# Streaming x through one core: main tiles of 128 positions of 4 batches in one loop over five groups, and a jump to a new instruction block at the start of the VectorE and ACT programs

## The chip, the cores and the metric

The kernel runs on one core of one Trainium2 chip. The metric is the time of one execution in device microseconds (us). The kernel before takes 630.12 us (median of 3 runs, 630.04 to 630.36). The profile is one execution recorded by the hardware profiler. Its span, from the first to the last instruction of the program, is about 2 us shorter than the time of the same run.

Names in the profile: DVE is VectorE, ACT is ScalarE, POOL is GpSimd, PE is TensorE (PEld its weight loads), SP is the engine that issues the DMAs of x; SPq and ACTq are DMA issues by SP and ACT. A packet is one contiguous piece that a DMA engine moves. The packet records do not name the engine, so a figure "for each DMA engine" is the total over 16.

## The reference

```python
def setup_inputs():
    B, S, D = 8, 2048, 4096
    return {"x": np.random.randn(B, S, D).astype(np.float32),
            "w": np.random.randn(D, 1).astype(np.float32)}

def reference(x, w):
    proj = (x @ w).squeeze(-1)                    # (8, 2048)
    cm = np.maximum.accumulate(proj, axis=1)      # running maximum along a row
    is_record = (proj >= cm).astype(np.float32)
    return np.cumsum(is_record, axis=1).astype(np.float32)
```

x is 268.4 MB and is read once. The output is 64 KB. Each element of x is used in one multiplication and one addition.

## The kernel before

Every position needs a dot product of 4096 elements. VectorE takes columns 0 to 2815 of a row in one instruction; POOL multiplies the other 1280 columns by w and ACT adds them up. A main tile is 8 MB: 128 partitions, each with four rows (64 KB) that follow each other in memory. There are three such buffers. The last 128 positions come as small pieces at the end, the tail pieces. SP issues a tile's DMA when VectorE and ACT have both finished the tile that was in its buffer before.

```python
    RS = (4, 4, 4, 3)            # rows of a partition in each of four groups
    R = RS[0]
    NS = 3                       # main buffers
    NG = len(RS); NL = NG - 1
    N = R * P                    # 512 positions in a group
    STARTS = [sum(RS[:g]) * P for g in range(NG)]
    S0 = sum(RS) * P             # the last 128 positions come as small pieces
    ...
        for g in range(NG):
            r = RS[g]
            for t in range(B):                       # one tile per batch
                i = SY.dma_start(
                    out=at(g, t)[:, : r * D],
                    in_=x[B - 1 - t, STARTS[g] : STARTS[g] + r * P, :].rearrange(
                        "(p r) d -> p (r d)", r=r
                    ),
                ).then_inc(xs[t], 16)
                u, n = user_before(g, t)
                if n:
                    i._wait_ge(*(free(u, n)))        # the buffer is free
                if g == t == 0:
                    A.dma_start(out=w_row, in_=...).then_inc(ws, 16)
    ... (small pieces of the last 128 positions, constants, broadcast of w by TensorE)

        def group_dots(r, g=0):                      # VectorE
            for t in range(B):
                b, xb = B - 1 - t, at(g, t)
                for j in range(r):
                    i = dot(xb[:, j * D : j * D + VC], w_v[:, :VC],
                            sum_v[:, j * B + b : j * B + b + 1])
                    if j == 0:
                        i._wait_ge(xs[t], 16)
                i.then_inc(fr[t], 1)

        with V.Fori(0, NL):
            group_scans(); V.sem_inc(psr, -3); group_dots(R)
        group_scans(); V.sem_inc(psr, -3); group_dots(RS[-1], NL)

        def group_products(r, g=0):                  # POOL, one instruction a row
            for t in range(B):
                for j in range(r):
                    xl = at(g, t)[:, j * D + VC : (j + 1) * D]
                    i = G.tensor_mul(out=xl, in0=xl, in1=w_sb).then_inc(pl, 1)
                    ...
        def group_sums(r, g=0):                      # ACT, each row waits for its product
            for t in range(B):
                for j in range(r):
                    i = add_up(at(g, t)[:, j * D + VC : (j + 1) * D], ...)._wait_ge(pl, j + 1)
                i.then_inc(fr[t], 1)
                A.sem_inc(pl, -r)
            ...
        def group_rows(r):                           # TensorE: sums to rows of the batches
            ...
            for j in range(r):
                for k, l in enumerate((sum_p, sum_v)):
                    i = T.matmul(out=ps[:B, j : r * P : r], lhsT=l[:, j * B : (j + 1) * B],
                                 rhs=identity, start=k == 0, stop=k == 1)
```

## Time and profile before

| | read from | value |
|---|---|---|
| time | timed runs | 630.12 us |
| span | page | 629.3 us |
| DMA queue 1, share of 16 engines' span | queue table | 98.9% |
| VectorE, POOL, ACT busy | page, part 1 | 65%, 59%, 29% |
| one 64 KB packet, median | packet records of the trace | 2.418 us |
| first x packet starts, last one ends | packet records | 1.98 us, 623.75 us |
| from the last x packet to the span's end | difference | 5.5 us |
| issue to landing of an 8 MB tile, median | DMA table | 45.0 us |

A tile is 128 packets of 64 KB on 16 DMA engines, so eight packets in a row on each: 8 x 2.418 = 19.34 us. The whole of x at the median packet times is 619.85 us for each engine. The stream as it ran is 621.8 us.

The lines below are from the page of the kernel before: busy time and share of the span of each engine; the DMA row of the 40 slices (9 is 90% busy or more); the queue table; the chain that ended last; three groups of instructions (busy us and mean ns of one, then idle us before them and what ended it); and the DMA issues (count, us from issue to landing).

```profile
span 629.3 us, 1140 instructions
...
PE 29.1 (5%) x96; PEld 13.5 (2%) x96; DVE 407.3 (65%) x294; ACT 181.2 (29%) x274; POOL 370.7 (59%) x149
...
DMA  9999999999999999999999999999999999999996
...
q1 hardware_dynamic: 6544, 268.50, 98.9%
...
DMA 16%; POOL 3%; DVE 2%; issue 1%; PE 1%; ACT 0%; SPq 0%
...
L124 DVE CUSTOM_DVE_ANT_0 xall<-xall,w_v 128x2816 f32<-128x2816 f32 (+1 forms) x129 | 385.5, 3041 | 181.8 <-DMA xall<-in_x_dram 181.8
L276 POOL TENSOR_TENSOR xall<-xall,w_sb 128x1280 f32<-128x1280 f32 x120 | 345.0, 2909 | 246.7 <-DMA xall<-in_x_dram 243.3
L130 ACT ACTIVATE xall<-xall 128x1280 f32<-128x1280 f32 (+2 forms) x130 | 162.9, 1253 | 428.6 <-POOL xall L276 408.3
...
xall<-in_x_dram SPq DMA_DIRECT2D x24, 45.0
```

The DMA row and the queue table say what bounds this kernel: the 16 engines are busy nearly all the time. The row alone would not show a short stop: e9 below stops for 1.6 us and has the same row. The packet records settle it, with 621.6 us busy of 621.8. The groups say that VectorE and POOL spend most of their idle time waiting for exactly these DMAs. The chain gives DMA only 16%, because it starts at 484 us and follows buffers through the engines that release them; it does not tell how full the queue is. The last line tells that: a tile lands 45.0 us after its issue and needs 19.3 us itself, so it was queued about 25.7 us ahead of its turn. I call this the lead: issue to landing, less 19.34 us.

The next lines are from the timeline of the kernel before, at the start (start us, us, engine, line, operation, count, idle time before and what ended it), and from one tile in the middle of the first group.

```profile
0.91 0.60 ACTq L178 DMA_DIRECT2D w<-in_w_dram  x1
...
0.97 1.34 SPq L168 DMA_DIRECT2D xall<-in_x_dram  x3
...
2.62 2.07 PE L224 MATMUL ps<-w,identity 8*128 8x512 f32 x2 [2.62 <-DMA w<-in_w_dram]
...
22.80 3.09 DVE L124 CUSTOM_DVE_ANT_0 xall<-xall,w_v 128x2816 f32<-128x2816 f32 x1 [0.67 <-DMA xall<-in_x_dram]
22.85 8.63 POOL L276 TENSOR_TENSOR xall<-xall,w_sb 128x1280 f32<-128x1280 f32 x3 [20.85 <-DMA xall<-in_x_dram]
```

```profile
81.65 3.09 DVE L124 CUSTOM_DVE_ANT_0 xall<-xall,w_v 128x2816 f32<-128x2816 f32 x1 [7.52 <-DMA xall<-in_x_dram]
81.69 11.49 POOL L276 TENSOR_TENSOR xall<-xall,w_sb 128x1280 f32<-128x1280 f32 x4 [8.13 <-DMA xall<-in_x_dram]
84.63 1.27 ACT L130 ACTIVATE xall<-xall 128x1280 f32<-128x1280 f32 x1 [9.67 <-POOL xall L276]
...
93.22 1.27 ACT L130 ACTIVATE xall<-xall 128x1280 f32<-128x1280 f32 x1 [1.50 <-POOL xall L276]
...
94.61 0.33 SPq L168 DMA_DIRECT2D xall<-in_x_dram  x1
```

w is there at 2.62 us, ahead of x. The first dot starts when the first tile has landed. In the middle of the run a tile starts its dots at 81.65, and SP issues the next DMA for that buffer at 94.61: 13 us from landing to reuse.

### The profile page before, as it was taken

How to read it: one execution, taken by the hardware profiler on the slowest of the kernel's cores; microseconds unless marked ns; L12 is line 12 of the kernel's file. 1: busy time of each engine (PE TensorE's matmuls, PEld its weight loads, DVE VectorE, ACT ScalarE, POOL GpSimd, SP SyncE). 2: the span in 40 equal slices, each digit the busy share in tenths (PEclk: the TensorE clock that was granted, in tenths of full speed). 3: DMA queues.
4: the chain of work that ended last, by engine and by line, in shares of the span. 5: the costliest groups of instructions: out<-in, count | busy, mean ns of one | idle time of the engine just before them, and what ended most of it. 6: DMA issues, size and time to landing. Idle time of an engine off the chain costs nothing. (4 is left out here: it accounts for less than half of the span.)

```text
span 629.3 us, 1140 instructions
## 1 busy us (share of the span) xinstructions
PE 29.1 (5%) x96; PEld 13.5 (2%) x96; DVE 407.3 (65%) x294; ACT 181.2 (29%) x274; POOL 370.7 (59%) x149
## 2 busy tenths in 40 slices
PE   8000000000020000000001000000002000000100
PEld 3000000000010000000000000000001000000000
DVE  0755775556766567755578655676556976655897
ACT  1222332223322233222233222332223232232254
POOL 0554675456765557745577555676557666555775
PEclk9999999999999999999996555555555555555565
DMA  9999999999999999999999999999999999999996
GB/s 401 400 467 400 446 421 425 442 437 429 442 425 450 417 450 417 459 408 458 408 458 408 458 408 458 408 459 408 462 418 438 416 447 441 413 447 444 404 425 248
DMA packets 6563, 268.54 MB, mean 427 GB/s; under 512 B 760, under 2 KB 1016, under 8 KB 1568
## 3 DMA queue, kind: packets, MB, share of 16 engines
q1 hardware_dynamic: 6544, 268.50, 98.9%
q10 hardware_dynamic: 16, 0.02, 0.0%
q14 instruction: 3, 0.02, 0.0%
HBM read 268.45 MB, written 0.07 MB: 427 GB/s over the span
## 5 line engine op out<-in xcount | busy, mean ns | idle before, releaser
L124 DVE CUSTOM_DVE_ANT_0 xall<-xall,w_v 128x2816 f32<-128x2816 f32 (+1 forms) x129 | 385.5, 3041 | 181.8 <-DMA xall<-in_x_dram 181.8
L276 POOL TENSOR_TENSOR xall<-xall,w_sb 128x1280 f32<-128x1280 f32 x120 | 345.0, 2909 | 246.7 <-DMA xall<-in_x_dram 243.3
L130 ACT ACTIVATE xall<-xall 128x1280 f32<-128x1280 f32 (+2 forms) x130 | 162.9, 1253 | 428.6 <-POOL xall L276 408.3
L312 PE MATMUL ps<-identity,small 128*8 128x128 f32 x60 | 13.0, 406 | 568.6 <-PEq L309 568.6
L130 ACT ACTIVATION_READ_ACCUMULATOR xall<-xall 128x1 f32 x130 | 24.2, 186 | 0.0
L336 POOL TENSOR_TENSOR xall<-xall,w_sb 128x1280 f32<-128x1280 f32 (+2 forms) x8 | 21.1, 2632 | 3.1 <-DMA xall<-in_x_dram 3.0
L312 PEld LDWEIGHTS ps<-identity,small 128*8 128x8 f32 x60 | 7.3, 125 | 575.4 <-issue 571.3
L140 DVE TENSOR_TENSOR_SCAN cm<-ps,cm,small 8x512 f32<-8x512 f32 (+3 forms) x8 | 7.0, 869 | 18.8 <-PE ps L312 18.4
L224 PE MATMUL w_v<-w,identity 8*128 8x512 f32 x14 | 12.1, 1056 | 0.0
L124 DVE DVE_READ_ACCUMULATOR2_ANT small<- 128x1 f32 x133 | 10.8, 81 | 0.0
L246 DVE MEMSET ps<- 8x512 f32 x1 | 0.5, 485 | 15.7 <-ACT w L235 15.7
L146 DVE TENSOR_TENSOR_SCAN cnt<-ps,cnt,small 8x512 f32<-8x512 f32 (+3 forms) x8 | 7.0, 870 | 0.3
L224 PEld LDWEIGHTS w_v<-w,identity 8*128 8x128 f32 x14 | 4.6, 332 | 7.3 <-issue 7.3
L143 DVE TENSOR_TENSOR ps<-ps,cm 8x512 f32<-8x512 f32 (+3 forms) x8 | 3.9, 487 | 0.3
L232 ACT COPY w_sb<-w_v 128x768 f32<-128x768 f32 x1 | 0.8, 799 | 11.4 <-PE w_v L224 11.4
L347 POOL TENSOR_TENSOR masked<-fold,small 128x4 f32<-128x4 f32 x8 | 1.6, 201 | 3.2 <-DVE small L124 3.2
L124 DVE CUSTOM_DVE_ANT_0 xall<-xall,w_v,small 128x480 f32<-128x480 f32 (+2 forms) x4 | 3.1, 810 | 0.2 <-DVE small L124 0.2
L357 PE MATMUL ps<-fold,masked 128*8 128x32 f32 x20 | 2.0, 235 | 25.3 <-ACT masked L352 17.7
L352 ACT ACTIVATE masked<-fold,small 128x4 f32<-128x4 f32 x10 | 3.0, 298 | 0.3
L336 POOL TENSOR_TENSOR xall<-xall,w 128x640 f32<-128x640 f32 (+1 forms) x2 | 2.3, 1137 | 0.1
L224 PE MATMUL ps<-w,identity 8*128 8x512 f32 x2 | 2.1, 1135 | 2.6 <-DMA w<-in_w_dram 2.6
L231 ACT ACT_TABLE_LOAD x1 | 1.3, 1283 | 2.7 <-DVE fold L242 2.7
(18 smaller groups left out, 5.3 us busy)
## 6 DMA issues: line engine op xcount, KB each, us to landing
xall<-in_x_dram SPq DMA_DIRECT2D x8, 6144.0 KB, 33.5
xall<-in_x_dram SPq DMA_DIRECT2D x6, 2048.0 KB, 42.4
xall<-in_x_dram SPq DMA_DIRECT2D x1, 1264.0 KB, 36.6
xall<-in_x_dram SPq DMA_DIRECT2D x1, 816.0 KB, 39.3
xall<-in_x_dram SPq DMA_DIRECT2D x1, 784.0 KB, 37.9
xall<-in_x_dram SPq DMA_DIRECT2D x2, 240.0 KB, 26.6
xall<-in_x_dram SPq DMA_DIRECT2D x1, 416.0 KB, 39.4
xall<-in_x_dram SPq DMA_DIRECT2D x24, 45.0
```

The source lines that it names most:

```text
L124: return V.tensor_tensor_reduce(out=xsl, in0=xsl, in1=wsl, scale=1.0, scalar=seed, op0=ALU.mult, op1=ALU.add, accum_out=dst,)
L130: return A.activation(out=xsl, in_=xsl, func=ACTF.Copy, accum_out=dst)
L140: V.tensor_tensor_scan(out=cm_, data0=src, data1=low, initial=cm0, op0=ALU.max, op1=ALU.max,)._wait_ge(psr, base).then_inc(psr, 1)
L143: V.tensor_tensor(out=src, in0=src, in1=cm_, op=ALU.is_ge)._wait_ge(psr, base + 1).then_inc(psr, 1)
L146: V.tensor_tensor_scan(out=cnt_, data0=src, data1=low, initial=cnt0, op0=ALU.add, op1=ALU.max,)._wait_ge(psr, base + 2).then_inc(cs, 1)
L224: i = T.matmul(out=dst, lhsT=identity[:NW, k : k + 1].to_broadcast([NW, P]), rhs=w_row, start=True, stop=True,).then_inc(bw, 1)
L276: i = G.tensor_mul(out=xl, in0=xl, in1=w_sb).then_inc(pl, 1)
L312: i = T.matmul(out=ps[:B, j : r * P : r], lhsT=l[:, j * B : (j + 1) * B], rhs=identity, start=k == 0, stop=k == 1,)
L336: G.tensor_mul(out=xl, in0=xl, in1=w_pool(*p))._wait_ge(xq[i], 16).then_inc(pl, 1)
L347: return eng.tensor_tensor(out=e, in0=by_b, in1=acc.to_broadcast([P, H]), op=ALU.mult)
L352: return A.activation(out=e, in_=by_b, func=ACTF.Copy, scale=acc)._wait_ge(pa, na).then_inc(ms, 1)
L357: return T.matmul(out=ps[:B, k * Q : (k + 1) * Q], lhsT=masked[:, n * B : (n + 1) * B], rhs=by_i, start=start, stop=stop,)
```

## The change

The intent: fewer and larger instructions on POOL, one loop for all main tiles instead of a loop and an unrolled rest, and instruction loops that begin at a block boundary. A main tile now holds 128 positions of four batches: partition 4q + b has rows 4q to 4q + 3 of batch b, still 64 KB of consecutive memory. A group is 384 positions of all eight batches (six tiles), and there are five groups. POOL multiplies a tile's four rows in one instruction (two and two in the last tile of a group); ACT starts after it. At a group's end POOL adds the two partial sums and spreads them with a mask, and TensorE makes rows of them with twelve small matmuls. The last main tile comes in two halves. VectorE and ACT jump to an address aligned to 128 instruction slots before anything else.

```diff
-    RS = (4, 4, 4, 3)
-    R = RS[0]
+    R = 4
     NS = 3
-    NG = len(RS)
+    H = 4
+    NC = 3
+    NT = NC * B // H
+    N = NC * P
+    NG = 5
+    STARTS = [g * N for g in range(NG)]
+    S0 = NG * N
...
+    for eng in (V, A):
+        eng.addr_align(128, 0, max_nops=0)
...
         for g in range(NG):
-            r = RS[g]
-            for t in range(B):
-                i = SY.dma_start(
-                    out=at(g, t)[:, : r * D],
-                    in_=x[B - 1 - t, STARTS[g] : STARTS[g] + r * P, :].rearrange(
-                        "(p r) d -> p (r d)", r=r
-                    ),
-                ).then_inc(xs[t], 16)
+            for t in range(NT):
+                b0, s0 = t % 2 * H, STARTS[g] + t // 2 * P
+                src = x[b0 : b0 + H, s0 : s0 + P, :].rearrange(
+                    "b (q r) d -> q b (r d)", r=R
+                )
...            (last tile of the last group: two halves, semaphores xs[t] and xh)
+                    i = SY.dma_start(out=at(t), in_=src).then_inc(xs[t], 16)
...
-                for j in range(r):
-                    xl = at(g, t)[:, j * D + VC : (j + 1) * D]
-                    i = G.tensor_mul(out=xl, in0=xl, in1=w_sb).then_inc(pl, 1)
+                rows = at(t).rearrange("p (r d) -> p r d", r=R)
+                n = R // 2 if t == NT - 1 else R
+                for j in range(0, R, n):
+                    xl = rows[:, j : j + n, VC:]
+                    i = G.tensor_mul(
+                        out=xl, in0=xl, in1=w_one.to_broadcast([P, n, PC])
+                    ).then_inc(pl, 1)
+                    landed(i, t, j)
+            G.tensor_tensor(out=sum_t, in0=sum_v, in1=sum_p, op=ALU.add)...
+            G.tensor_tensor(out=gmask..., in0=sum_t..., in1=by_b..., op=ALU.mult)...
...
-                for k, l in enumerate((sum_p, sum_v)):
+                for c in range(NC):
+                    k = j * NC + c
                     i = T.matmul(
-                        out=ps[:B, j : r * P : r], lhsT=l[:, j * B : (j + 1) * B],
-                        rhs=identity, start=k == 0, stop=k == 1,
+                        out=ps[:B, c * P + j : (c + 1) * P : R],
+                        lhsT=gmask[:, k * B : (k + 1) * B],
+                        rhs=by_i, start=True, stop=True,
                     )
```

More of the change, by code (lines that the diff above doesn't have):

```diff
@@ L41 @@
     NW = D // WC
-    RS = (4, 4, 4, 3)
-    R = RS[0]
+    R = 4
     NS = 3
-    NG = len(RS)
-    NL = NG - 1
-    N = R * P
-    STARTS = [sum(RS[:g]) * P for g in range(NG)]
-    S0 = sum(RS) * P
-    assert S0 + P == S
+    H = 4
+    Q = P // H
+    NC = 3
[4 more added lines that the diff above has]
+    S0 = NG * N
+    assert S0 + P == S and NT % NS == 0
     VC = 2816
@@ L53 @@
     CV = 3584
-    H = 4
-    Q = P // H
     LAST = [
@@ L87 @@
     w_sb = sb([P, PC], "w_sb")
-    cm = sb([B, N], "cm")
-    cnt = sb([B, N], "cnt")
+    cm = sb([B, N + P], "cm")
+    cnt = sb([B, N + P], "cnt")
+    gmask = sb([P, R * NC * B], "gmask")
     masked = sb([P, 10 * B], "masked")
@@ L102, in cut @@
         return small[:, off[0] - n : off[0]]
-    sum_v, sum_p = cut(R * B), cut(R * B)
+    sum_v, sum_p, sum_t = (cut(R * NT) for _ in range(3))
     acc_v, acc_p = cut(B - 2), cut(B - 2)
@@ L112, in sem @@
         return tc.alloc_semaphore(f"{name}_{next(ns)}")
-    xs = [sem("xs") for _ in range(B)]
-    fr = [sem("fr") for _ in range(B)]
+    xs = [sem("xs") for _ in range(NT)]
+    fr = [sem("fr") for _ in range(NT)]
     xq = [sem("xq") for _ in TILES]
-    ws, bw, wc, cs, od, oe, psr, pd, pl, go, sd, pa, con, fo, ms, p7, mg, pg, ml = (
-        sem(n) for n in "ws bw wc cs od oe psr pd pl go sd pa con fo ms p7 mg pg ml".split()
+    ws, bw, wc, cs, od, oe, psr, pd, pl, xh, sd, pa, con, fo, ms, p7, mg, pg, ml, mk = (
+        sem(n) for n in "ws bw wc cs od oe psr pd pl xh sd pa con fo ms p7 mg pg ml mk".split()
     )
@@ L148, in scans, with at, col_of @@
         )._wait_ge(psr, base + 2).then_inc(cs, 1)
-    def at(g, t):
-        return xbuf[(t if g < NL else t + NS - 1) % NS]
+    def at(t):
+        return xbuf[t % NS]
     def user_before(g, t):
-        if t >= NS:
-            return t - NS, g + 1
-        if g == NL:
-            return B - NS + t, g
-        return max(u for u in range(B) if u % NS == t), g
-    def free(u, n):
-        return (p7, n) if u == B - 1 else (fr[u], 2 * n)
+        return (t - NS, g + 1) if t >= NS else (t + NT - NS, g)
+    def free(u, n):
+        return (p7, n) if u == NT - 1 else (fr[u], 2 * n)
+    def col_of(t, j):
+        return (j * NC + t // 2) * 2 + t % 2
+    for eng in (V, A):
+        eng.addr_align(128, 0, max_nops=0)
     with tc.tile_critical(no_gpsimd_drain=True):
         for g in range(NG):
-            r = RS[g]
-            for t in range(B):
-                i = SY.dma_start(
-                    out=at(g, t)[:, : r * D],
-                    in_=x[B - 1 - t, STARTS[g] : STARTS[g] + r * P, :].rearrange(
-                        "(p r) d -> p (r d)", r=r
-                    ),
-                ).then_inc(xs[t], 16)
-                u, n = user_before(g, t)
+            for t in range(NT):
[3 more added lines that the diff above has]
+                )
+                half = R // 2 * D
+                last = t == NT - 1
+                u, n = user_before(g, t)
+                if last and g == NG - 1:
+                    i = SY.dma_start(
+                        out=at(t)[:, :half], in_=src[:, :, :half]
+                    ).then_inc(xs[t], 16)
+                    SY.dma_start(
+                        out=at(t)[:, half:], in_=src[:, :, half:]
+                    ).then_inc(xh, 16)
+                else:
+                    i = SY.dma_start(out=at(t), in_=src).then_inc(xs[t], 16)
+                    if last:
+                        SY.sem_inc(xh, 16)
                 if n:
-                    i._wait_ge(*(free(u, n)))
+                    i._wait_ge(*free(u, n))
                 if g == t == 0:
@@ L182 @@
                     SY.dma_start(
-                        out=out[:, STARTS[g - 1] : STARTS[g]], in_=cnt
+                        out=out[:, STARTS[g - 1] : STARTS[g]], in_=cnt[:, :N]
                     )._wait_ge(cs, g + 1).then_inc(od, 16)
         def slot(m):
-            if m < NS:
-                return None, xbuf[m][:, RS[-1] * D :]
-            u = B - NS if m < 2 * NS else B - NS + 1
-            return u, at(NL, u)[:, (m % NS) * D : (m % NS + 1) * D]
-        freed = {None}
+            u = NT - NS + m // 4
+            return u, at(u)[:, m % 4 * D : (m % 4 + 1) * D]
+        freed = set()
         for i, (m, c0, c1, _, _) in enumerate(TILES):
@@ L215 @@
         G.memset(masked, 0.0).then_inc(con, 1)
-        G.memset(cm[:, N - 1 :], NEG).then_inc(con, 1)
-        G.memset(cnt[:, N - 1 :], 0.0).then_inc(con, 1)
+        G.memset(cm[:, N - 1 : N], NEG).then_inc(con, 1)
+        G.memset(cnt[:, N - 1 : N], 0.0).then_inc(con, 1)
         T.wait_ge(con, 2)
@@ L246 @@
         V.memset(ps[:B, :N], LOW)._wait_ge(wc, 3).then_inc(psr, 1)
-        def group_scans(r=R):
-            n = r * P
-            scans(cm[:, :n], cnt[:, :n], ps[:B, :n], cm[:, N - 1 :], cnt[:, N - 1 :])
-        def group_dots(r, g=0):
-            for t in range(B):
-                b, xb = B - 1 - t, at(g, t)
-                for j in range(r):
-                    i = dot(
-                        xb[:, j * D : j * D + VC], w_v[:, :VC],
-                        sum_v[:, j * B + b : j * B + b + 1],
-                    )
-                    if j == 0:
-                        i._wait_ge(xs[t], 16)
-                i.then_inc(fr[t], 1)
@@ L264, with group_scans, landed @@
-        with V.Fori(0, NL):
+        def group_scans():
+            scans(
+                cm[:, :N], cnt[:, :N], ps[:B, :N], cm[:, N - 1 : N], cnt[:, N - 1 : N]
+            )
+        def landed(i, t, j):
+            if j == 0:
+                i._wait_ge(xs[t], 16)
+            elif t == NT - 1 and j == R // 2:
+                i._wait_ge(xh, 16)
+        with V.Fori(0, NG):
             group_scans()
             V.sem_inc(psr, -3)
-            group_dots(R)
-        group_scans()
-        V.sem_inc(psr, -3)
@@ L270 @@
-        group_dots(RS[-1], NL)
-        def group_products(r, g=0):
-            for t in range(B):
-                for j in range(r):
-                    xl = at(g, t)[:, j * D + VC : (j + 1) * D]
-                    i = G.tensor_mul(out=xl, in0=xl, in1=w_sb).then_inc(pl, 1)
-                    if j == 0:
-                        i._wait_ge(xs[t], 16)
-        G.wait_ge(wc, 3)
-        with G.Fori(0, NL):
-            group_products(R)
-            G.wait_ge(pg, 1).then_inc(pg, -1)
-        group_products(RS[-1], NL)
@@ L286, in group_sums @@
-        def group_sums(r, g=0):
-            for t in range(B):
-                b = B - 1 - t
-                for j in range(r):
-                    i = add_up(
-                        at(g, t)[:, j * D + VC : (j + 1) * D],
-                        sum_p[:, j * B + b : j * B + b + 1],
-                    )._wait_ge(pl, j + 1)
+            for t in range(NT):
+                xb = at(t)
+                for j in range(R):
+                    c = col_of(t, j)
+                    i = dot(
+                        xb[:, j * D : j * D + VC], w_v[:, :VC], sum_v[:, c : c + 1]
+                    )
+                    landed(i, t, j)
+                i.then_inc(fr[t], 1)
@@ new lines @@
+        G.wait_ge(wc, 3)
+        w_one = w_sb.rearrange("p (o c) -> p o c", o=1)
+        with G.Fori(0, NG):
+            for t in range(NT):
+                rows = at(t).rearrange("p (r d) -> p r d", r=R)
[5 more added lines that the diff above has]
+                    ).then_inc(pl, 1)
+                    landed(i, t, j)
+            G.tensor_tensor(
+                out=sum_t, in0=sum_v, in1=sum_p, op=ALU.add
+            )._wait_ge(fr[NT - 1], 2).then_inc(mk, 1)
+            G.tensor_tensor(
+                out=gmask.rearrange("p (k b) -> p k b", b=H),
+                in0=sum_t.rearrange("p (k o) -> p k o", o=1).to_broadcast(
+                    [P, R * NT, H]
+                ),
+                in1=by_b.rearrange("p (o b) -> p o b", o=1).to_broadcast(
+                    [P, R * NT, H]
+                ),
+                op=ALU.mult,
+            )._wait_ge(mk, 1).then_inc(mk, 1)
+            G.wait_ge(pg, 1).then_inc(pg, -1)
@@ L294, in group_sums @@
+        with A.Fori(0, NG):
+            for t in range(NT):
+                for j in range(R):
+                    c = col_of(t, j)
+                    i = add_up(
+                        at(t)[:, j * D + VC : (j + 1) * D], sum_p[:, c : c + 1]
+                    )
+                    if j == 0 or t == NT - 1 and j == R // 2:
+                        i._wait_ge(pl, 1)
+                    if j == R - 1 or t == NT - 1 and j == R // 2 - 1:
+                        A.sem_inc(pl, -1)
                 i.then_inc(fr[t], 1)
-                A.sem_inc(pl, -r)
@@ L296, in group_sums @@
             A.wait_ge(pd, 1).then_inc(pd, -1)
-        with A.Fori(0, NL):
-            group_sums(R)
-        group_sums(RS[-1], NL)
-        def group_rows(r):
-            T.wait_ge(fr[B - 1], 2).then_inc(p7, 1)
-            T.sem_inc(fr[B - 1], -2)
-            if r == R:
-                for s in xs:
-                    T.sem_inc(s, -16)
-                T.sem_inc(pg, 1)
+        with T.Fori(0, NG):
+            T.wait_ge(mk, 2).then_inc(p7, 1)
+            T.sem_inc(mk, -2)
+            T.sem_inc(fr[NT - 1], -2)
+            for s in (*xs, xh):
+                T.sem_inc(s, -16)
+            T.sem_inc(pg, 1)
@@ L309, in group_rows @@
             T.wait_ge(od, 16).then_inc(od, -16)
-            for j in range(r):
-                for k, l in enumerate((sum_p, sum_v)):
+            for j in range(R):
+                for c in range(NC):
+                    k = j * NC + c
                     i = T.matmul(
-                        out=ps[:B, j : r * P : r], lhsT=l[:, j * B : (j + 1) * B],
-                        rhs=identity, start=k == 0, stop=k == 1,
-                    )
-                    if j == r - 1:
-                        i.then_inc((pd, psr)[k], 1)
@@ L319 @@
-        with T.Fori(0, NL):
-            group_rows(R)
-        group_rows(RS[-1])
+                        out=ps[:B, c * P + j : (c + 1) * P : R],
+                        lhsT=gmask[:, k * B : (k + 1) * B],
+                        rhs=by_i, start=True, stop=True,
+                    )
+                    if k == 0:
+                        i.then_inc(pd, 1)
+            i.then_inc(psr, 1)
         nv = npool = na = 0
@@ L376 @@
             if m == 2:
-                group_scans(RS[-1])
+                group_scans()
             if m == 4:
```

## The prediction

> **What bounds the kernel now.** The DMA stream of x. The queue table gives queue 1 98.9% of the span; the slice row shows the DMA engines at 90% or more in 39 of 40 slices. In the packet records a 64 KB packet takes 2.418 us, so 16 engines move 433.7 GB/s; the Trainium skill, "DMA: Bandwidth & Descriptors", section "Where 436 GB/s comes from", puts the ceiling at 435.2, and the trace agrees. First x packet 1.98 us after the span's start, last one ended at 623.76: 621.8 us of stream, 621.6 busy. At median packet times it would take 619.9; the rest is slow packets, 0.6 us in the first ones, 1.1 us between 30 and 118 us. After the last packet 5.5 us remain: last dots, turn matmul, scans, output DMA, exit barrier. VectorE (65%), POOL (59%) and ACT (29%) are not limits.
>
> The DMA table shows 45.0 us from issue to landing of an 8 MB tile whose transfer takes 8 x 2.418 = 19.3 us: each DMA is queued 25 us before its turn.
>
> **What the change does.**
> - Same bytes. 30 tiles of 8 MB instead of 24 of 8 MB and 8 of 6 MB: 1024 packets of 48 KB (1.815 us) become 768 of 64 KB, 0.1 us less per engine. One tile is halved (32 KB packets): +0.05 us. A partition's row stays 64 KB contiguous.
> - POOL multiplies four rows in one instruction, about 4 x 2.91 = 11.6 us; ACT (1.46 us a row) starts only after it: release 17.4 us after landing instead of 13.1. Issue to landing falls from 45 to about 40.5 us, twice the 19.3 needed. No stall.
> - Group end: POOL adds and masks (under 1 us), TensorE does 12 small matmuls instead of 16 wider ones (3.2 us before), scans take about 2.6 us instead of 3.2. All inside the slack.
> - The last main tile in halves brings VectorE to the tail pieces about 3 us earlier, but the timeline shows VectorE and POOL waiting for DMA there already. No gain; the last pieces and their 5.5 us stay.
> - The jump costs VectorE and ACT a branch, possibly an instruction fetch. If ACT's small load of w slips behind the first x packets, the first dots start after 22.8 us, but need to start only by about 40. No effect.
> - SP issues three-dimensional tail pieces in 0.6 us, main tiles in 0.4: first packet up to 0.2 us later.
>
> **Prediction.** What is removed is off the critical path. Sum: -0.1, +0.05, +0.2; slow packets may change by -1.5 to +1. I expect 629.9 us, 8 in 10 between 628.7 and 631.1; faster by over 2% 0.01, within 2% 0.97, slower by over 2% 0.02.
>
> **Signs.** Right: 64 KB packets at 2.42 us, first packet at 2.0 to 2.3, stream near 621.5, 5.5 us behind it, issue to landing near 40, fewer POOL instructions. Wrong: packets over 2.45 us throughout, gaps in the slice row, VectorE idle beside tiles that have landed.
>
> **What would make it wrong.** Four batches lie 32 MB apart. The same page, section "Latency and other measured facts", reports much lower rates for row pitches of large powers of two between HBM tensors. The tail pieces already read this way at 0.611 us per 16 KB (429 GB/s), so I give it little weight. Or instruction fetches behind full queues could stall an engine near the end: some us at most.

## More of the kernel before

Most runs agree within 0.5 us.

## The result, and the profile after

The changed kernel takes 630.33 us (median of 4 runs, 630.22 to 630.45) against 630.24 us of the kernel before in the same rounds. The ratio is 1.0001, with a 95% interval of 0.9984 to 1.0018. Ratios are the mean time of one kernel's runs over that of the other's of the same rounds, so they are not quite the ratio of the medians quoted. They come out when the first run of each kernel is left out; for e6, whose runs scatter, that makes 1.0394 instead of 1.0378 with all runs.

The profiled run of before was one of its slower ones: it took 631.05 us and its span is 629.3 us, while the spans of its timed runs in the later rounds are 628.1 to 628.9. So the 1.0 us between the two profiled spans is not a gain. Nor does the granted TensorE clock matter here: it was 0.773 in this profile and 1.000 in the one after, but TensorE is busy for 5% of the span, and runs of the kernel before at 0.64 to 0.89 all took 629.9 to 630.7 us.

The lines below are from the page of the changed kernel, in the order of those of before.

```profile
span 628.3 us, 1242 instructions
...
PE 23.2 (4%) x156; PEld 12.7 (2%) x156; DVE 406.9 (65%) x297; ACT 171.7 (27%) x274; POOL 360.7 (57%) x74
...
DMA  9999999999999999999999999999999999999996
...
q1 hardware_dynamic: 6416, 268.50, 98.9%
...
DMA 71%; POOL 18%; ACT 7%; issue 2%; DVE 1%; SPq 0%; PE 0%
...
L125 DVE CUSTOM_DVE_ANT_0 xall<-xall,w_v 128x2816 f32<-128x2816 f32 (+1 forms) x129 | 385.5, 3041 | 167.7 <-DMA xall<-in_x_dram 167.7
L291 POOL TENSOR_TENSOR xall<-xall,w_sb 128x5120 f32<-128x5120 f32 (+1 forms) x35 | 332.2, 9498 | 242.1 <-DMA xall<-in_x_dram 216.8
L131 ACT ACTIVATE xall<-xall 128x1280 f32<-128x1280 f32 (+2 forms) x130 | 161.3, 1241 | 428.3 <-POOL xall L291 411.3
...
xall<-in_x_dram SPq DMA_DIRECT2D x29, 41.7
```

The DMA row and the queue share are as before. POOL has 74 instructions instead of 149; a product of four rows takes 11.05 us in the timeline, against 4 x 2.909 = 11.64 (the mean of 9498 ns mixes these with the products of two rows). The chain now gives DMA 71%, POOL 18% and ACT 7%. It reads like another kernel, but nothing of it became a limit: it follows each buffer through POOL and ACT for the whole run. Issue to landing is 41.7 us, a lead of 22.4 us instead of 25.7.

The timeline of the changed kernel, at the start and at a tile in the middle:

```profile
0.96 42.99 SPq L185 DMA_DIRECT2D xall<-in_x_dram  x4
...
1.34 2.30 ACTq L191 DMA_DIRECT2D w<-in_w_dram  x1
...
11.45 2.07 PE L235 MATMUL ps<-w,identity 8*128 8x512 f32 x2 [11.45 <-DMA w<-in_w_dram]
...
27.21 11.03 POOL L291 TENSOR_TENSOR xall<-xall,w_sb 128x5120 f32<-128x5120 f32 x1 [25.21 <-ACT w L246]
...
30.09 3.05 DVE L125 CUSTOM_DVE_ANT_0 xall<-xall,w_v 128x2816 f32<-128x2816 f32 x1
```

```profile
81.62 3.09 DVE L125 CUSTOM_DVE_ANT_0 xall<-xall,w_v 128x2816 f32<-128x2816 f32 x1 [7.25 <-DMA xall<-in_x_dram]
81.67 11.05 POOL L291 TENSOR_TENSOR xall<-xall,w_sb 128x5120 f32<-128x5120 f32 x1 [8.33 <-DMA xall<-in_x_dram]
...
92.75 1.27 ACT L131 ACTIVATE xall<-xall 128x1280 f32<-128x1280 f32 x1 [14.26 <-POOL xall L291]
...
96.52 1.25 ACT L131 ACTIVATE xall<-xall 128x1280 f32<-128x1280 f32 x1
...
97.89 0.53 SPq L185 DMA_DIRECT2D xall<-in_x_dram  x1
```

The load of w is issued at 1.34 us instead of 0.91, so after SP's first DMA of x (0.96) and no longer before it, and the issue takes 2.30 us instead of 0.60. Packets of x now go first: the packets of w move only at 8.0 us, after two packets of x, and the small packets that end the load come at 10.5 to 10.9 us, after a third. TensorE waits for them until 11.45, and the first dot starts at 30.09 us although the first tile has landed at 23.6. In the middle, the tile that starts at 81.62 is free at 97.89, after 16.3 us instead of 13.

The packet records give the sum for both kernels and for the experiments that follow (us). "Lost" is the time of the x packets above the median for their size, for each DMA engine.

| run | first x packet | lost in the first 16 packets | lost later | last x packet ends | after it | w moves at | first dot |
|---|---|---|---|---|---|---|---|
| before | 1.98 | 0.64 | 1.13 | 623.75 | 5.50 | 1.9 | 22.80 |
| after | 2.39 | 0.95 | 0.31 | 622.91 | 5.41 | 8.0 | 30.09 |
| e1, no jump | 2.37 | 0.88 | 0.22 | 623.40 | 5.49 | 1.9 | 23.80 |
| e2, jump only | 1.99 | 0.63 | 0.21 | 623.09 | 5.50 | 7.4 | 30.29 |
| e3, row products | 2.38 | 0.88 | 0.06 | 623.15 | 5.51 | 7.8 | 30.16 |
| e4, one batch a tile | 1.98 | 0.68 | 0.34 | 622.41 | 5.48 | 7.4 | 29.53 |
| e5, after again | 2.36 | 0.93 | 0.16 | 622.74 | 5.45 | 8.0 | 30.05 |

Every run is the same sum: about 2 us of start, 620 us of packets at their median, 0.8 to 1.8 us lost, 5.5 us of end. The first three add up to the end of the last packet within 0.6 us, so smaller differences than that should not be read from the table. The 6.1 us by which w is late are in none of these terms.

### The profile page after: what moved, and what is told of

It reads as the page before. It is cut to its first block, busy times and chain, and to the rows that moved or that the text cites. A ratio compares the mean times of both kernels' runs of the same rounds, so it can differ in the third digit from the quotient of the medians.

```text
span 628.3 us, 1242 instructions
## 1 busy us (share of the span) xinstructions
PE 23.2 (4%) x156; PEld 12.7 (2%) x156; DVE 406.9 (65%) x297; ACT 171.7 (27%) x274; POOL 360.7 (57%) x74
## 4 chain that ended last, share of the span: by engine, by line
DMA 71%; POOL 18%; ACT 7%; issue 2%; DVE 1%; SPq 0%; PE 0%
DMA xall<-in_x_dram 71%; POOL xall L291 18%; ACT xall L131 7%; POOL xall L357 1%; DVE xall L125 0%; SPq L185 0%; PE ps L378 0%; ACT masked L373 0%; SPq L207 0%; POOL masked L368 0%; DVE cm L141 0%; DVE cnt L147 0%; DVE ps L144 0%; SPq L463 0%; DVE small L125 0%
## 5 line engine op out<-in xcount | busy, mean ns | idle before, releaser
L291 POOL TENSOR_TENSOR xall<-xall,w_sb 128x5120 f32<-128x5120 f32 (+1 forms) x35 | 332.2, 9498 | 242.1 <-DMA xall<-in_x_dram 216.8
L335 PE MATMUL ps<-fold,gmask 128*8 128x32 f32 x120 | 7.2, 240 | 563.7 <-PEq L331 563.7
L141 DVE TENSOR_TENSOR_SCAN cm<-ps,cm,small 8x384 f32<-8x384 f32 (+2 forms) x9 | 6.9, 765 | 23.6 <-PE ps L335 23.2
L335 PEld LDWEIGHTS ps<-fold,gmask 128*8 128x8 f32 x120 | 6.5, 114 | 565.9 <-issue 565.9
L147 DVE TENSOR_TENSOR_SCAN cnt<-ps,cnt,small 8x384 f32<-8x384 f32 (+2 forms) x9 | 6.9, 766 | 0.3
L144 DVE TENSOR_TENSOR ps<-ps,cm 8x384 f32<-8x384 f32 (+2 forms) x9 | 3.9, 435 | 0.3
## 6 DMA issues: line engine op xcount, KB each, us to landing
xall<-in_x_dram SPq DMA_DIRECT2D x29, 41.7
```

What stands on the lines that cost most here:

```text
L141: V.tensor_tensor_scan(out=cm_, data0=src, data1=low, initial=cm0, op0=ALU.max, op1=ALU.max,)._wait_ge(psr, base).then_inc(psr, 1)
L144: V.tensor_tensor(out=src, in0=src, in1=cm_, op=ALU.is_ge)._wait_ge(psr, base + 1).then_inc(psr, 1)
L147: V.tensor_tensor_scan(out=cnt_, data0=src, data1=low, initial=cnt0, op0=ALU.add, op1=ALU.max,)._wait_ge(psr, base + 2).then_inc(cs, 1)
L291: i = G.tensor_mul(out=xl, in0=xl, in1=w_one.to_broadcast([P, n, PC])).then_inc(pl, 1)
L335: i = T.matmul(out=ps[:B, c * P + j : (c + 1) * P : R], lhsT=gmask[:, k * B : (k + 1) * B], rhs=by_i, start=True, stop=True,)
```

## The experiments

The theories were these. A: the DMA stream alone sets the time, and everything else is hidden behind DMAs that are queued ahead. B: two effects cancel; the new tiles gain some microseconds and the late w loses them. C: reading four batches that lie 32 MB apart costs or gains something in HBM. D: the engines are nearer to the limit than the profile says. E: the late w would cost nothing, however many buffers there are.

### e1: the tiles without the jump

```diff
-    for eng in (V, A):
-        eng.addr_align(128, 0, max_nops=0)
```

> The changed kernel without the jump of VectorE and ACT; the tiles of four batches stay. Theory A (the DMA stream alone sets the time, all else is hidden under queued DMAs): the small load of w again moves before the x packets, at about 1.9 us instead of 8.0, the first dot starts near 22.5 us instead of 30.1, the first x packet comes at about 2.2 us (0.2 for the three-dimensional issue stays), and the time stays within 1 us of 630.2. Rival B (two effects cancel: the new tiles gain some us, the late w loses them): 3 to 7 us faster than before, 623 to 627.

Measured: 630.98 us (630.86 to 631.16) against 630.43 us; ratio 1.0010 (0.9997 to 1.0024). w moves at 1.9 us again. The first dot starts at 23.80, not near 22.5, because the first tile lands later than I had allowed. The first x packet comes at 2.37, not 2.2. Theory B asked for 623 to 627 us and falls.

### e2: the jump without the tiles

```diff
 (kernel before)
+    for eng in (V, A):
+        eng.addr_align(128, 0, max_nops=0)
```

> The kernel before with the jump alone. Theory A: w is late by about 6 us, the first dot starts near 30 us instead of 22.8, the instruction fetches in mid run (105, 117 and 488 us) are gone or fewer, and the time stays within 1 us of 630.2. Rival B (cancelling effects): 3 to 7 us slower than before, 633 to 637.

Measured: 630.55 us (630.39 to 631.00) against 630.43; ratio 1.0004 (0.9991 to 1.0018). w moves at 7.4 us and the first dot starts at 30.29. So the jump alone makes w late, and it costs nothing that can be measured. The expectation of fewer instruction fetches was wrong: five packets of 8 KB on the instruction queue fall into the span, at 1.8, 1.9, 487, 560 and 569 us, against three before (105, 117 and 488 us). In the changed kernel there are two, both at the start.

### e3: POOL's product row by row again

```diff
-                n = R // 2 if t == NT - 1 else R
+                n = 1
...
-                    if j == 0 or t == NT - 1 and j == R // 2:
-                        i._wait_ge(pl, 1)
-                    if j == R - 1 or t == NT - 1 and j == R // 2 - 1:
-                        A.sem_inc(pl, -1)
+                    i._wait_ge(pl, j + 1)
                 i.then_inc(fr[t], 1)
+                A.sem_inc(pl, -R)
```

> The changed kernel with POOL's product and ACT's wait row by row again, as before; right result. Theory A: a buffer is free about 13 us after landing instead of 16.3, issue to landing goes back from 41.7 to about 45 us, the time stays within 1 us of 630.2. Rival B (the large product gains what something else loses): slower by some us.

Measured: 630.91 us (630.51 to 630.96) against 630.43; ratio 1.0009 (0.9993 to 1.0024). Issue to landing is 45.0 us again. Each buffer comes free 3.3 us earlier and the time does not change, so POOL's and ACT's 25% of the chain after the change was not a limit: what they no longer take, the DMA spends in the queue.

### e4: one batch in a tile (wrong result)

```diff
-                b0, s0 = t % 2 * H, STARTS[g] + t // 2 * P
-                src = x[b0 : b0 + H, s0 : s0 + P, :].rearrange(
-                    "b (q r) d -> q b (r d)", r=R
-                )
+                n8 = g * NT + t
+                s0 = n8 // B * R * P
+                src = x[n8 % B, s0 : s0 + R * P, :].rearrange(
+                    "(p r) d -> p (r d)", r=R
+                )
```

> The changed kernel, but each main tile is read as 512 rows of one batch, contiguous 8 MB with a two-dimensional pattern, as before (wrong result on purpose). Theory A: 64 KB packets stay at 2.418 us, the first x packet comes about 0.2 us earlier than 2.39 because SP issues in 0.4 instead of 0.6 us, the time within 1 us. Rival C (four batches 32 MB apart cost or gain something in HBM that another part hides): the sum of slow packets changes by more than 2 us per DMA engine, and the time by as much.

Measured: 630.09 us (629.78 to 630.25) against 630.43; ratio 0.9995 (0.9980 to 1.0010). 64 KB packets stay at 2.418 us. The first x packet comes at 1.98 instead of 2.39, and the first sixteen lose 0.68 instead of 0.95: together the start of the stream is 0.7 us earlier, which is all that the four-batch source is seen to cost. The changed kernel itself was not in these rounds; e1 and e3, which keep the four-batch source and were, took 630.98 and 630.91 us, and their ranges do not overlap with that of e4, so the timed runs fit a cost of this size. Only half of the 0.41 us by which the first packet is later is the longer issue (0.63 us instead of 0.40); the rest is unexplained. Theory C asked for more than 2 us and falls.

### e5: the changed kernel again

> The changed kernel unaltered, once more, beside the kernel before on this chip. In the profiles so far the four-batch tiles cost about 0.4 us before the first x packet and 0.25 us in the first sixteen packets, and nothing later. Theory A: 0 to 0.7 us slower than before, ratio 0.999 to 1.002. Rival B and C: a ratio outside of that.

Measured: 630.30 us (630.17 to 631.02) against 630.20; ratio 1.0004 (0.9991 to 1.0018), as expected.

### e6 and e7: two buffers instead of three, with and without the jump

The first dot is 7 us late and no time is lost. If the third buffer hides it, it should show when that buffer is gone.

```diff
-    NS = 3
+    NS = 2
```

> The changed kernel with two main buffers instead of three; right result. It takes away the spare tile behind which theory A says the late w is hidden. Theory A: in the steady state a buffer is free 16.3 us after landing, under the 19.3 us of a transfer, so the stream stays full there; at the start the first buffer comes free at 43.4 us (first dot at 30.1 because w is late) while the second tile has landed at about 42.2, so the stream stops there once for 2 to 3 us: 632 to 634 us. Rival D (the third buffer is needed all the time, engines are nearer to the limit than the profile says): 650 us and more. Rival E (the late w costs nothing whatever the buffers): within 1 us of the changed kernel.

> Two buffers and no jump. Theory A: w is early, the first buffer is free at about 40.1 us, before the second tile has landed, so the stream does not stop, or for less than 0.7 us: 630 to 631.5 us, that is 2 to 3 us faster than with the jump. Rival D: 650 and more with or without the jump. Rival E: no difference to the run with the jump.

Measured: 653.97 us with the jump (650.88 to 657.11; ratio 1.0394, 1.0362 to 1.0426) and 652.94 us without (649.71 to 655.89; ratio 1.0361, 1.0325 to 1.0396). Both expectations of theory A are far off. The size is that of theory D, but its reason is not: a buffer is still free 16.3 us after landing, as before, and VectorE and POOL still wait for DMA.

What happens is in the semaphore records of the trace: a tile's semaphore gets 16 increments, taken here as one from each DMA engine when its part has landed. The table is for main tiles issued between 100 and 535 us; spread is the time from the first of the 16 to the last.

| run | time | issue to landing, median | the shortest | spread, median | one tile to the next, mean |
|---|---|---|---|---|---|
| after | 630.33 | 41.69 | 41.60 | 0.39 | 19.32 |
| e6, two buffers | 653.97 | 23.93 | 22.39 | 2.01 | 20.02 |
| e7, two buffers, no jump | 652.94 | 24.38 | 22.51 | 2.41 | 20.07 |
| e9, two buffers, rows | 633.01 | 25.62 | 24.78 | 0.60 | 19.33 |
| e10, two buffers, rows, no jump | 630.78 | 25.66 | 24.79 | 0.65 | 19.32 |

With two buffers the lead is 22.39 - 19.34 = 3.05 us for the tile with the shortest time. Read directly, SP's issue comes 3.0 to 6.2 us (median 3.3) before the last of the 16 increments of the tile in flight. The stream does not stay full with that lead: the engines drift apart by about one packet, a tile counts as landed only when the last engine is done, and a tile takes 0.7 us longer. Thirty tiles make 21 us. The profiled run of e6 is its fastest (650.9 us); its packet records show, for each engine, 9.0 us lost in slow packets after the first sixteen and about 10 us idle, 2.9 of them between 40 and 50 us, where the late w stops the stream. Those 3 us are hardly a reserve: e8 below shows that a tile issued into an empty queue takes 22.2 to 22.5 us to land. Theory A left out this time to start and to land; counted in, it would still leave about 1.4 us (e8), so why an engine falls behind by a packet is not shown.

### e9 and e10: two buffers with row products, with and without the jump

This gives the lead back without the third buffer: with POOL's product row by row a buffer is free after 13 us.

```diff
 (changed kernel)
-    NS = 3
+    NS = 2
 (and the edit of e3; e10 also that of e1)
```

> Two buffers, jump, and POOL's product row by row. The two-buffer runs cost 23 us, not 2: there the next tile was queued only 3.05 us before the one in flight ended, and the sixteen DMA engines drifted apart by a whole packet (2 to 2.9 us). Theory A2 (the reserve that counts is the time a tile is queued ahead; 3 us is too little, and the product of four rows made it so): with rows a buffer is free about 13 us after landing, the lead is 6.3 us, the stream stays full after the start, and only the late w stops it once, for 1.5 to 3 us: 632 to 634 us. Rival F (two buffers are too few whatever the lead): 645 and more.

> Two buffers, row by row, no jump. Theory A2: w is early, the first buffer is free at about 37 us, 5 us before the second tile ends, no stop at all: 630 to 631.5 us, 1.5 to 3 us faster than with the jump. Rival F: 645 and more. Rival E (the late w costs nothing): no difference to the run with the jump.

Measured: 633.01 us with the jump (632.77 to 633.27; ratio 1.0045, 1.0030 to 1.0060) and 630.78 without (630.62 to 631.03; ratio 1.0010, 0.9994 to 1.0025). Both are where theory A2 put them, and rivals E and F fall. The lead of 6.3 us is enough with two buffers. (The row products change the shape of POOL's work along with the lead; with three buffers, in e3, that shape alone gained nothing. The lead alone was not varied.) With two buffers the product of four rows costs 21 to 22 us (e6 against e9, e7 against e10), and the late w costs 2.2 us (e9 against e10). In e6 against e7 the scatter of 6 us hides that.

The stretches of the run show both, in the view by windows. Its columns are the stretch, its length, busy us and count of PE, PEld, DVE, ACT and POOL, the granted clock, the DMA share and GB/s. First e6, two buffers with the jump:

```profile
41.00:61.00 20.00, 0.00 (x0) 0.00 (x0) 13.31 (x10) 7.53 (x12) 11.05 (x1) 1.00 0.89 367
...
320.00:580.00 260.00, 2.88 (x48) 2.59 (x48) 162.58 (x110) 69.83 (x110) 145.01 (x19) 1.00 0.99 423
```

The same for e7, two buffers without the jump:

```profile
41.00:61.00 20.00, 0.00 (x0) 0.00 (x0) 12.12 (x8) 5.12 (x8) 11.05 (x1) 1.00 0.98 419
...
320.00:580.00 260.00, 2.88 (x48) 2.59 (x48) 162.58 (x110) 66.07 (x103) 145.06 (x19) 1.00 0.98 413
```

Then e9, two buffers and rows with the jump:

```profile
41.00:61.00 20.00, 0.00 (x0) 0.00 (x0) 13.23 (x10) 5.45 (x8) 11.50 (x4) 1.00 0.90 370
...
320.00:580.00 260.00, 2.88 (x48) 2.59 (x48) 171.16 (x117) 75.06 (x112) 159.33 (x60) 1.00 1.00 432
```

And e10, two buffers and rows without the jump:

```profile
41.00:61.00 20.00, 0.00 (x0) 0.00 (x0) 12.12 (x8) 5.45 (x8) 11.51 (x4) 1.00 0.97 419
...
320.00:580.00 260.00, 2.88 (x48) 2.58 (x48) 171.21 (x117) 75.08 (x111) 159.31 (x60) 1.00 1.00 435
```

From 41 to 61 us e6 and e9 move 367 and 370 GB/s, e7 and e10 419: this is the one stop that the late w causes. From 320 to 580 us e6 and e7 move only 423 and 413 GB/s, and e9 and e10 are back at 432 and 435: this is the short lead. Such a view is coarse: one round of 16 packets of 64 KB is 1.05 MB, which is 52 GB/s in 20 us and 4 GB/s in 260 us, so 432 and 435 are the same, and the share of 0.97 in the first window of e10 is no stop. The packet records give the stop itself: between 40 and 50 us the engines idle for 2.9 us in e6, 1.6 in e9, and not at all in e7 and e10. The queue waits do not tell the runs apart: SP waits for ACT for 472 us in e6, 405 in e9 and 442 in e10, against 436 in the changed kernel. The length of such waits tells nothing of whether the stream is full.

### e8: three more dots a tile on VectorE

```diff
                     landed(i, t, j)
+                i.then_inc(dq, 1)
+                for j in range(3):        # sums go to spare columns
+                    i = dot(xb[:, j * D : j * D + VC], w_v[:, :VC], spare[...])
+                    if j == 0:
+                        i._wait_ge(dq, 1)
+                V.sem_inc(dq, -1)
                 i.then_inc(fr[t], 1)
```

> The changed kernel with three spare dots a tile on VectorE (right result): 7 x 3.06 = 21.4 us a tile, over the 19.33 us of its transfer, so VectorE must take over as the bound. Theory A: a group takes 6 x 21.4 plus about 7 us of group end on VectorE, 135 us, five of them 677, plus 30 at the start and some 33 for the tail pieces: 730 to 750 us, and gaps in the DMA row. If time were set by something else than max(DMA, slowest engine): near 630, or over 790.

Measured: 727.51 us (two runs), 2.5 us under the expected range; right result. From the page of e8, its span, the busy times (us, share, instructions) and the DMA row:

```profile
span 725.4 us, 1452 instructions
...
PE 23.3 (3%) x156; PEld 12.7 (2%) x156; DVE 677.7 (93%) x477; ACT 171.8 (24%) x274; POOL 360.1 (50%) x74
...
DMA  9999999998799999878998995999989968999820
```

VectorE is busy for 93% of the span and the DMA row has gaps: VectorE is the bound as expected, so the model of "the slower of stream and engine" holds on both sides, as long as tiles are queued early enough (e6 breaks it). The range was too high, at least in part because I counted 3.06 us for a dot; most dots that follow each other start every 3.01 us.

e8 also measures what a tile needs when nothing is queued ahead of it. The first line is the issue of a DMA and of the one after it; the second is POOL's start on the tile of the first:

```profile
185.06 21.72 SPq L188 DMA_DIRECT2D xall<-in_x_dram  x2
...
207.63 11.04 POOL L303 TENSOR_TENSOR xall<-xall,w_sb 128x5120 f32<-128x5120 f32 x1 [14.51 <-DMA xall<-in_x_dram]
```

The tile before had landed at 180.4 us, so this one was issued into an empty queue, and it landed at 207.56, 22.5 us after its issue. Three tiles between 100 and 535 us came so late, 4.4 to 4.8 us after the landing of the tile before; they took 22.2 to 22.5 us. Their first packet starts 1.3 us after the issue, their first packets take about 3.3 us instead of 2.42, and the last increment comes 0.3 us after the last packet. So the figure that I call lead is already 2.9 to 3.2 us for a tile with no lead at all, and the 3.05 us of e6 are of that size. An estimate from these numbers: in e6 the next tile's packets can start 3.05 - 0.3 - 1.3 = 1.4 us before the tile in flight is done, less than one packet of 2.42 us. How a short lead becomes drift stays open: in e8 tiles are issued only 1.2 us (median) before the tile in flight lands, the stream stops between them, and the spread is still 0.65 us.

### e11: fewer bytes, the same work (wrong result)

```diff
-                    i = SY.dma_start(out=at(t), in_=src).then_inc(xs[t], 16)
+                    c = R * D if g == 0 else (R - 1) * D
+                    i = SY.dma_start(
+                        out=at(t)[:, :c], in_=src[:, :, :c]
+                    ).then_inc(xs[t], 16)
```

> The changed kernel, but from the second group on 23 main tiles load only three of their four rows (wrong result on purpose, the fourth row is an old one); all work of the engines stays. Theory A: 23 tiles x 128 packets x (2.418 - 1.815) us / 16 = 111 us less: 519 us, 516 to 522, since a tile's 14.5 us are still above the 12.2 us of VectorE and the lead is about 12 us with three buffers. Rival D (engines or waits share the bound): over 530.

Measured: 519.67 us (two runs), 0.7 us from the 519 expected. The engines do the same work in 17.5% less time. From the page of e11, its span, the busy times and the DMA row:

```profile
span 517.7 us, 1242 instructions
...
PE 23.2 (4%) x156; PEld 12.7 (2%) x156; DVE 406.2 (78%) x297; ACT 171.8 (33%) x274; POOL 360.9 (70%) x74
...
DMA  8999999999999999999999999999999999999995
```

This is the strongest evidence for theory A: bytes taken from the stream are returned in full, while work moved, merged or delayed on the engines is not.

### e12: the first tile in four DMAs

An attempt at a version that beats both: win back the later first packet.

```diff
+                elif g == t == 0:
+                    for b in range(H):
+                        i = SY.dma_start(
+                            out=xall[b:P:H, : R * D],
+                            in_=x[b, :P, :].rearrange("(q r) d -> q (r d)", r=R),
+                        ).then_inc(x0 if b else xs[t], 16)
 (VectorE and POOL wait once for x0 >= 48)
```

> The changed kernel with the first tile loaded by four two-dimensional DMAs, one for each batch (right result): an attempt to win back the later start of the stream. Theory A: the first x packet comes at about 1.98 us instead of 2.37, the first sixteen packets lose about 0.65 instead of 0.9 us, so the profile's stream ends some 0.5 us earlier than in the changed kernel, at 622.0 to 622.5, and the time is 629.5 to 630.2, within the noise of before. If the later start came from elsewhere: first packet still at 2.37.

Measured: 630.36 us (630.04 to 630.53) against 630.15; ratio 1.0002 (0.9988 to 1.0016). It failed: the first packet comes at 2.32 us, the first sixteen lose 0.91 us, the stream ends at 623.16. SP takes 0.56 to 0.59 us to issue each of these DMAs although their patterns are two-dimensional, against 0.40 for a contiguous 8 MB tile. So "three dimensions" was not the reason for the longer issue. What is, stays open; a tile that takes its partitions from consecutive memory in order is the only form seen at 0.40.

## Why the prediction was right

The time was right: 629.9 us predicted, 630.33 measured, inside 628.7 to 631.1. Point by point:

- The bound. "Everything removed is off the critical path" is shown by e11 (fewer bytes, 111 us less) and by e1, e2 and e3, in which parts are taken out and the time stays within 0.6 us. The new group end, the halved last tile and the single loop were not taken out one by one. 64 KB in 2.418 us on 16 engines is 433.7 GB/s in both kernels, within half a per cent of the ceiling that the prediction names, which leaves at most that half per cent for any new tiles to gain in the middle of the stream.
- Packet sizes: right. The x packets at their medians are 619.85 us before and 619.82 after.
- Release and lead: right in direction, off in size. Predicted 17.4 us to release and 40.5 us from issue to landing; measured 16.3 and 41.7. The product of four rows takes 11.05 us, not 11.6, and ACT's rows follow each other every 1.25 us, not 1.46, when none waits for a product.
- Group end: right. From the page and its groups, POOL's sum and mask take 0.6 us, TensorE is busy 1.4 us a group instead of 3.2, and the scans take 2.6 us instead of 3.2. VectorE starts the tail pieces at 590.1 us instead of 594.0.
- "Twice the 19.3 needed": the conclusion was right, the threshold was not. e6 has 22.4 to 25.6 us (median 23.9), more than 19.3, and loses about 24 us; e10 has 25.7 and loses nothing that can be measured. A tile with nothing ahead of it needs 22.2 to 22.5 us (e8), so that was the figure to compare with. What counts is the lead over the tile in flight: 3 us is too little, 6.3 us is enough, and the changed kernel has 22.4.
- The late w: right. It starts to move 6.1 us later, TensorE gets it 8.8 us later, and the first dot comes 7.3 us later. VectorE then stands idle for 6.5 us beside a tile that has landed, which the prediction lists among the signs that it is wrong; here it was harmless. It is hidden because the third tile is still on its way: the first buffer is free at 43.4 us, and the third tile lands at 62.2. e9 and e10 show the 2.2 us that it costs when that tile is not there. Whether the first dot could start as late as 40 us was not tested.
- The first packet: 0.2 us predicted, 0.41 measured, and 0.3 more lost in the first sixteen packets. Against it stand 0.8 us fewer lost later; but the amount lost later also differs between runs with the same tiles (1.13 before, 0.21 in e2; 0.31 and 0.16 in two profiles of the changed kernel), so it is put down to no part of the change.
- The last tenths are luck. The three listed terms add 0.15 us to 630.12, which is 630.27; the prediction took off 0.35 more for fewer slow packets. The timed runs are 0.1 us apart (630.24 and 630.33 in the same rounds), and neither the 0.7 us at the start, where 0.2 had been expected, nor a gain of slow packets can be seen in them.
- Batches 32 MB apart: no loss in HBM (e4). The instruction fetches near the end did not come in the changed kernel.
- The end of 5.5 us stayed: 5.41 us.

No version beats both. e4 has the lowest time and a wrong result; the differences that remain are at the start of the stream, 0.7 us of 630.

## What to carry to other kernels

When the DMA engines have no gaps, count bytes and packets first, and expect changes to the engines' work to move the time by nothing until the lead of the queue is used up. Read the lead from the issue-to-landing time less the transfer's own time, and keep several microseconds of it: a buffer that comes free "in time" by 3 us cost 3.8% here, and 6 us cost nothing. A tile with nothing queued ahead of it already showed 2.9 to 3.2 us of this figure (e8). Neither the chain of waits nor the sum of waits on the issuing queue tells whether such a stream is full; the packet times and the landing interval do.

## What the Trainium skill lacked or had wrong

- "DMA: Bandwidth & Descriptors", section "Rules for kernel authors", says to issue a DMA early so that it overlaps with compute, and gives no lead. Here, with a lead of 3.05 us at the least over a transfer of 19.34 us, the engines landed 2 us apart (median; up to 2.8) and the kernel was 3.8% slower (e6); with 6.3 us they stayed within 0.9 us (e9, e10). A tile issued into an empty queue landed after 22.2 to 22.5 us (e8).
- The same page, section "Queues, rings and completion order", says that an engine round-robins between its queues at packet granularity, but not what a small load then waits for. Here the 2 KB packets of w, issued at 1.34 us, moved at 8.0 us, after two 64 KB packets of x (3.4 and 2.42 us), and the load was complete only after a third, at 10.5 to 10.9 us.
- The same page, section "Latency and other measured facts", has a row on HBM row pitches of large powers of two, measured between HBM tensors. It doesn't say whether loads into SBUF suffer too. In the one pattern tried here, four rows 32 MB apart and 64 KB in a row, packets stayed at 2.418 us, as with contiguous tiles (e4).
- No page that I found gives the issue time of a large DMA on SP by its pattern. For the first two DMAs of a run it was 0.40 to 0.41 us for a contiguous 8 MB tile (before, e4) and 0.56 to 0.63 us where the partitions come from four batches, whether as one DMA (after) or four (e12); later in the run 0.33 and 0.53 us.
- "Runtime: NRT & Kernel Launch", section "Instruction fetch mechanics", says that instructions come in blocks of 16 KiB. The fetches in these traces are packets of 8,192 bytes, single ones in the kernel before (105, 117 and 488 us). Whether two of them make up a block is not shown.
